# A two-block transformer on one core: the expert stage's banks, row fetches and weight pieces, and one more weight panel

## The chip, the cores and the metric

The kernel runs on one core of a Trainium2 chip. The metric is the device time of one execution in microseconds (us), lower is better; of several runs the median counts.

## The reference, cut to what matters

Two blocks work on 512 tokens of 1024 numbers, in float32. The first is attention of four kinds and a feed-forward layer. The second is a recurrent branch, a sparse attention branch, a cross attention and, last, a layer of 32 experts; then a final norm. The change touches the first product of the second block, `rmsnorm(h) @ w_in`, and the expert layer with all that follows:

```
p_grp, grp  = top_k(softmax(xt @ w_rg + b_rg), 1)          # one group of four
p_e, e_loc  = top_k(softmax(e_logits of that group), 2)    # two experts of its eight
gate        = p_grp * p_e / sum(p_e)
hid = silu(xb @ w_gate[e]) * (xb @ w_up[e])                # 1024 -> 512, xb: the rows routed to e
y[token] += (hid @ w_down[e]) * gate                       # 512 -> 1024
out = rmsnorm(h + y, norm_final)
```

Each of 512 tokens goes to two experts, so there are 1024 routed rows.

## The kernel before, in words

The code is one Python program that writes out every instruction. A scheduler orders the instructions of each engine when the kernel is built, by the program's order and by when its own model has an instruction's inputs and buffers ready; on the chip each engine then runs its own list in that order, and waits where an input is late. All weight loads are issued by SyncE (SP).

**Panels.** Outside the experts a float32 matrix product is made of three products of split numbers (`mm3`, lines 131 to 135). `panel` (line 106) loads 512 KB of weights in two pieces into `wraw` (three buffers in the pool `wp`, line 124), and splits each piece into a high part (ScalarE, line 125) and a low part (VectorE or GpSimd, line 128), which go to a tile `w`. The pool `wp` has three `w` tiles; another pool, `fw`, has two, which `panel` takes when `filling` is set; with `last=True` it takes the pool named in `self.wx`.

**The second block begins** in `rwkv_prep` (line 1218). `fm_halves` (line 158) makes four panels of `w2f`, and then multiplies them by the first 256 tokens, all four, and after that by the other 256. Each panel is 24 matmuls of 256 columns a half. The fourth panel's `w` tile is a `wp` tile that the first panel holds until its second half is done. Behind the four follow the panels of `mix(12)` and `mix(13)`.

**Router and slots.** `Router` finds each token's two experts block by block of 128 tokens: `R` (line 1858) is the token's place in its expert's list of up to 64, `A` and `Gt` are choice and gate. `full` counts experts that overflow, `gates` (line 1871) makes `Gt`. Then `Slots` (line 1937) is made: `ti` holds token numbers, gates and norm factors, in split parts. `gather(n)` for a pair of experts compares `R` with the place numbers (`OH`, line 1954, four VectorE operations), multiplies `OH` with `ti` (line 1959, four matmuls of 68 columns), turns the first column into a row number (lines 1961 to 1964; a place that is not taken becomes row 0), fetches 128 rows of 4 KB by an indirect DMA of GpSimd (line 1966), and copies gates and factors (lines 1970 to 1975). The first two pairs' rows are fetched before the experts begin, the others two pairs ahead.

**Experts.** `Experts.load` (line 1908) loads one of an expert's six pieces of 1 MB as two DMAs of 512 KB (line 1919). There are 192 such pieces and 16 tiles for them (`MW_AT`), of four pools; a tile is loaded again when its matmuls are done. `moe` (line 1990) goes over 16 pairs of experts. Two experts work side by side on TensorE: each takes 64 of the 128 columns of the array, so the matmuls of lines 2008 and 2024 come as 128x64, two at a time. For one pair: gate and up, 64 matmuls of 512 columns into the two banks `f` (line 2008); `silu_mul` (ScalarE line 1894, VectorE lines 1895 and 1896) makes `hid`; four transposes (line 2014, 128x128) and a copy make `hT`; the down product, 2 x 16 matmuls into `s` (line 2024), each half then scaled by the gate into `yhi` and `ylo` (lines 2027, 2028); eight transposes of the next pair's rows (line 1985). After every second pair the results are scattered to the tokens: eight sums of four matmuls 128x128 by 512 columns (line 1934), in the banks `pv`, `acc`, `s`, `s`, each added to `x` by VectorE (line 2045).

**Banks.** PSUM has eight banks: `f` two, `s` two, `tp` two, `pv` one, `acc` one.

**The end.** The last scatter is joined with the final norm (lines 2053 to 2075): two chains, each for two token blocks, of squares, a reciprocal root (`rsqrt`, line 192), products and stores.

Of the kernel before, what the change touches and what calls it, by code (L numbers as in the profile page):

```python
# [13 lines left out]
I32 = mybir.dt.int32  # L14
# [31 lines left out]
class Core:  # L46
# [1171 lines left out]
def rwkv_prep(K, pool, hhi, hlo, Mt, VA, eC, xg, kbd, red, bvd):  # L1218
# [6 lines left out]
    first = K.fm_halves([a["w2f"][4 + i] for i in range(4)], ("f", "f", "acc", "s"), hhi, hlo)  # L1225
# [673 lines left out]
class Experts:  # L1899
# [8 lines left out]
    def load(self):  # L1908
        e, w = self.order[self.n]
        at = MW_AT[self.n % len(MW_AT)]  # L1910
        self.n += 1
        if at == "wp":
            t = self.K.wp.tile([P, 2, 1024], F32R, name="w", bufs=W0).bitcast(F32)
        elif at == "mm":
            t = self.pools[at].tile([P, 2, 1024], F32R, name="mw", bufs=4).bitcast(F32)
        else:
            t = self.pools[at].tile([P, 2, 1024], F32, name="mw", bufs=MW_AT.count(at))
        for h in range(2):
            (self.K.nc.gpsimd if self.n in SWQ else self.K.nc.sync).dma_start(t[:, h], self.K.a["wexp"][e * 6 + w, :, h * 1024:(h + 1) * 1024])
        return [t[:, h, c * 512:c * 512 + 512] for h in range(2) for c in range(2)]  # L1920
# [16 lines left out]
class Slots:  # L1937


    def __init__(self, K, keep, xnd, Gt, R, r4, pool, mc):  # L1940
        self.K, self.xnd, self.R, self.pool, self.mc = K, xnd, R, pool, mc
        nc = K.nc
        self.ti = ti = keep.tile([P, 4, 68], F32R, name="ti")
        nc.vector.tensor_copy(ti[:, :, 0:2], mc["tok2"].rearrange("p (b c) -> p b c", b=4))
        K.split(ti[:, :, 2:34], ti[:, :, 34:66], Gt)
        K.split(ti[:, :, 66:67], ti[:, :, 67:68], r4[:, :, None])
        self.ready = [self.gather(0), self.gather(1)]

    def gather(self, n):
        K, nc, pool = self.K, self.K.nc, self.pool  # L1950
        e0 = 2 * n
        OH = pool.tile([P, 4, P], F32R, name="OH", bufs=2)
        for b in range(4):
            nc.vector.tensor_tensor(OH[:, b].rearrange("p (e s) -> p e s", e=2),
                                    self.mc["iota64"][:, None, :].to_broadcast([P, 2, 64]),
                                    self.R[:, b, e0:e0 + 2, None].to_broadcast([P, 2, 64]), op=OP.is_equal)
        pt = K.acc("tp")
        for b in range(4):
            nc.tensor.matmul(pt[:, :68], OH[:, b], self.ti[:, b], start=b == 0, stop=b == 3)
        tg = K.sm.tile([P, 4], F32, name="tg")  # L1960
        nc.vector.tensor_copy(tg[:, 0:1], pt[:, 0:1])

        row = K.sm.tile([P, 1], I32, name="row")
        nc.vector.tensor_scalar(row, pt[:, 0:1], -1.0, 0.0, op0=OP.add, op1=OP.max)
        xs = pool.tile([P, D], F32, name="xs", bufs=2)
        nc.gpsimd.indirect_dma_start(xs, None, self.xnd, bass.IndirectOffsetOnAxis(ap=row[:, 0:1], axis=0))  # L1966
        for s in range(2):
            hs = slice(64 * s, 64 * s + 64)
            e = e0 + s
            nc.vector.tensor_copy(tg[hs, 1:2], pt[hs, 2 + e:3 + e])  # L1970
            nc.vector.tensor_add(tg[hs, 1:2], tg[hs, 1:2], pt[hs, 34 + e:35 + e])
        nc.vector.tensor_copy(tg[:, 2:3], pt[:, 66:67])
        nc.vector.tensor_add(tg[:, 2:3], tg[:, 2:3], pt[:, 67:68])
# [16 lines left out]
def moe(K, x, slots, weights, pool, mc, out):  # L1990
# [3 lines left out]
    for q in range(8):  # L1994
        for pr in range(2):
# [5 lines left out]
            G, U = K.acc("f"), K.acc("f")  # L2001
# [57 lines left out]
    os_ = [K.acc(t) for t in ("pv", "acc", "f", "f")]  # L2059
# [4 lines left out]
    for p in range(2):  # L2064
        for b in (2 * p, 2 * p + 1):
            nc.scalar.activation(j[:, h1], os_[b], AF.Square, accum_out=ss[:, b, 1:2])
        s = ss[:, 2 * p:2 * p + 2]
        nc.vector.tensor_add(s[:, :, 0], s[:, :, 0], s[:, :, 1])
        r = K.rsqrt(s[:, :, 0], 1.0 / D, 1e-6, 2)
        for i, b in enumerate((2 * p, 2 * p + 1)):  # L2070
            rows = out[b * P:(b + 1) * P]
            nc.scalar.activation(x[:, b, h0], x[:, b, h0], AF.Copy, scale=r[:, i:i + 1])
            nc.sync.dma_start(rows[:, h0], x[:, b, h0])
            nc.vector.scalar_tensor_tensor(x[:, b, h1], os_[b], r[:, i:i + 1], g[:, h1], op0=OP.mult, op1=OP.mult)
            nc.sync.dma_start(rows[:, h1], x[:, b, h1])
# [64 lines left out]
def block2(K, h3, xd, out):  # L2140
# [140 lines left out]
    weights = Experts(K, {"keep": keep, "mm": mp})  # L2281

# [41 lines left out]
    K.ws.close()  # L2324
    upto, ni = router.full(keep)
    Gt = router.gates(keep)
# [3 lines left out]
    slots = Slots(K, keep, xnd, Gt, router.R, r4, K.pool(E, "slots"), mc)  # L2330
# [65 lines left out]
```

## Time and profile before

| what | us |
|---|---|
| median of 3 runs (range) | 2228.69 (2226.29 to 2232.9) |
| the profiled execution, its own time | 2238.75 |
| its span on the core | 2237.0 |
| TensorE busy in that span | 2086.9 (93%) |

The profile is of one execution. Times in it count from the start of its span; what lies around the span is 1.75 us. Engines: PE is TensorE's matmul, PEld its weight load, DVE VectorE, ACT ScalarE, POOL GpSimd, SP SyncE; a q behind the name is the engine's own queue. `L135` is a line of the kernel before. PEclk is TensorE's granted clock as a share of full speed.

### The profile page before, as it was taken

To read this page: it belongs to the slowest core of one execution; us is meant where nothing else is said; L and a number is where in the kernel's file an instruction comes from. 1 tells how busy PE (TensorE), PEld (TensorE's weight loads), DVE (VectorE), ACT (ScalarE), POOL (GpSimd) and SP (SyncE) were. 2 spreads that over 40 slices of the span, in tenths; PEclk is the share of its full clock that TensorE was granted. 3 is DMA by queue.
4 is the path that set the end of the run, shared out by engine and by line. 5 is a ranking of instruction groups with operands and counts; after the bars stand their busy time and mean duration, and the time that the engine had idled before them with its cause. 6 is when DMAs were issued, how large, how long until landed. Compare 5 with 4: busy or idle time off the path is not lost.

```text
span 2237.0 us, 28592 instructions
## 1 busy us (share of the span) xinstructions
PE 2086.9 (93%) x10252; PEld 1476.5 (66%) x10252; DVE 1074.4 (48%) x2554; ACT 712.5 (32%) x1507; POOL 485.6 (22%) x391
## 2 busy tenths in 40 slices
PE   7999899998999999979988999999997999999997
PEld 5777676686888888867777867777875433333332
DVE  5272226427764545475877656555445322222223
ACT  4253334433353434234532235543441110000102
POOL 2312331233133222233331121232131000000000
PEclk9899999999999999999998799999998999999999
DMA  5512332256242332133334342485257999999994
GB/s 174 162 47 67 94 97 73 67 173 230 73 138 96 98 99 95 58 112 107 101 116 108 105 162 91 156 260 167 94 187 264 403 416 413 413 415 414 413 415 182
DMA packets 203370, 411.39 MB, mean 184 GB/s; under 512 B 49192, under 2 KB 67752, under 8 KB 203096
## 3 DMA queue, kind: packets, MB, share of 16 engines
q1 hardware_dynamic: 200632, 400.08, 51.0%
q0 software_dynamic: 2592, 9.44, 1.1%
q8 instruction: 82, 1.34, 0.3%
q14 instruction: 64, 0.52, 0.1%
HBM read 371.46 MB, written 33.13 MB: 181 GB/s over the span
## 4 chain that ended last, share of the span: by engine, by line
PE 68%; DVE 12%; DMA 7%; issue 3%; ACT 3%; POOL 2%; SPq 0%; DVEq 0%; ACTq 0%; POOLq 0%
PE f L135 23%; PE f L2008 10%; PE s L2024 6%; PE acc L135 6%; PE s L135 6%; PE tp L135 2%; POOL w L128 2%; PE pv L269 1%; PE tp L261 1%; PE s L1934 1%; DMA wraw<-w2f 1%; PE pv L135 1%; ACT w L125 1%; DMA wraw<-wout 1%; PE pv L1934 1%
## 5 line engine op out<-in xcount | busy, mean ns | idle before, releaser
L128 POOL TENSOR_TENSOR w<-wraw,w 128x512 fp32r<-128x512 f32 x310 | 407.2, 1325 | 1074.1 <-ACT w L125 962.0
L125 ACT CAST w<-wraw 128x512 fp32r<-128x512 f32 (+1 forms) x446 | 261.6, 617 | 242.2 <-issue 51.7
L135 PE MATMUL f<-hhi,w 128*128 128x512 f32 (+1 forms) x832 | 281.0, 410 | 2.0 <-ACT w L125 0.7
L128 DVE TENSOR_TENSOR w<-wraw,w 128x512 fp32r<-128x512 f32 (+1 forms) x136 | 116.3, 856 | 189.6 <-ACT w L125 186.5
L2008 PE MATMUL f<-mw,xT 128*64 128x512 f32 x832 | 206.8, 594 | 0.0
L135 PE MATMUL f<-h2hi,w 128*128 128x512 f32 (+1 forms) x672 | 203.7, 384 | 0.3 <-POOL w L128 0.3
L135 PEld LDWEIGHTS f<-hhi,w 128*128 128x128 f32 x832 | 161.8, 200 | 35.1 <-issue 3.2
L135 PE MATMUL acc<-hhi,w 128*128 128x512 f32 (+1 forms) x512 | 169.3, 398 | 4.9 <-ACT w L125 1.9
L135 PE MATMUL f<-hlo,w 128*128 128x512 f32 (+1 forms) x416 | 170.0, 409 | 0.2 <-DVE hlo L187 0.2
L2008 PEld LDWEIGHTS f<-mw,xT 128*64 128x64 f32 x832 | 65.5, 137 | 124.6 <-issue 117.7
L135 PEld LDWEIGHTS f<-h2hi,w 128*128 128x128 f32 x672 | 125.2, 188 | 25.6 <-POOL w L128 0.5
L135 PE MATMUL f<-h2lo,w 128*128 128x512 f32 (+1 forms) x336 | 129.0, 384 | 0.0
L2024 PE MATMUL s<-mw,hT 128*64 128x512 f32 x416 | 121.8, 600 | 3.3 <-ACT hT L174 1.9
L135 PEld LDWEIGHTS acc<-hhi,w 128*128 128x128 f32 x512 | 96.3, 191 | 28.5 <-issue 4.3
L1966 POOL DMA_INDIRECT xs<-xnd,row x16 | 15.2, 953 | 423.3 <-DVE wraw L2000 171.0
L135 PE MATMUL acc<-hlo,w 128*128 128x512 f32 (+1 forms) x256 | 101.3, 396 | 0.0
L135 PEld LDWEIGHTS f<-hlo,w 128*128 128x128 f32 x416 | 83.1, 200 | 16.2 <-issue 1.4
L1895 DVE SCALAR_TENSOR_TENSOR hid<-hid,f 128x512 f32<-128x512 f32 x16 | 11.0, 688 | 160.3 <-ACT hid L1894 160.3
L1894 ACT ACTIVATE hid<-f,tg 128x512 f32<-128x512 f32 x16 | 11.0, 688 | 204.1 <-PE f L2008 204.1
L2024 PEld LDWEIGHTS s<-mw,hT 128*64 128x64 f32 x416 | 33.2, 136 | 59.6 <-issue 51.5
L135 PEld LDWEIGHTS f<-h2lo,w 128*128 128x128 f32 x336 | 63.1, 188 | 12.3
L2027 ACT ACTIVATE yhi<-s,tg 128x512 fp32r<-128x512 f32 x32 | 22.0, 688 | 150.8 <-PE s L2024 150.8
(743 smaller groups left out, 3991.4 us busy)
## 6 DMA issues: line engine op xcount, KB each, us to landing
mw<-wexp SPq DMA_DIRECT2D x310, 512.0 KB
w<-wexp SPq DMA_DIRECT2D x72, 512.0 KB
wraw<-wup SPq DMA_DIRECT2D x88, 256.0 KB
wraw<-w2f SPq DMA_DIRECT2D x76, 256.0 KB
wraw<-wgate SPq DMA_DIRECT2D x64, 256.0 KB
wraw<-wdown SPq DMA_DIRECT2D x44, 256.0 KB
wraw<-w1f SPq DMA_DIRECT2D x40, 256.0 KB
gated<-gt SPq DMA_DIRECT2D x28, 256.0 KB
```

Of the source, the lines that this page charges most:

```text
L125: nc.scalar.copy(hi[:, s], raw)
L128: eng.tensor_sub(lo[:, s], raw, hi[:, s].bitcast(F32))
L135: self.nc.tensor.matmul(out, l, r, start=start and i == 0, stop=stop and i == 2)
L261: nc.tensor.transpose(pt[:, off:off + P], Pt[s][i][:, j * P:(j + 1) * P], K.ident)
L269: one = lambda s: nc.tensor.matmul(o[64 * s:64 * s + 64, j * P:], v_of(j, s), ptS[s][:, at[j]:at[j] + n], start=start and j == 0, stop=sto ...
L1894: nc.scalar.activation(t, G, AF.Tanh, scale=half)
L1895: nc.vector.scalar_tensor_tensor(t, t, 1.0, G, op0=OP.add, op1=OP.mult)
L1934: K.nc.tensor.matmul(o, CT[:, b * P:(b + 1) * P], y[:, hs], start=start and i == 0, stop=i == len(items) - 1)
L1966: nc.gpsimd.indirect_dma_start(xs, None, self.xnd, bass.IndirectOffsetOnAxis(ap=row[:, 0:1], axis=0))
L2008: nc.tensor.matmul(o[64 * s:64 * s + 64], xT[:, kk, 64 * s:64 * s + 64], ws[s][k], start=kk == 0, stop=kk == 7)
L2024: nc.tensor.matmul(o[64 * s:64 * s + 64], hT[:, c, 64 * s:64 * s + 64], ws[s][c], start=c == 0, stop=c == 3)
L2027: nc.scalar.activation(yhi[:, hs], o, AF.Copy, scale=tg[:, 1:2])
```

## The change

- `fm_halves` takes `extra`: the last panel or panels take their `w` tile from `K.wx`, which is set to `fw` around the call in `rwkv_prep`. The four panels no longer share three tiles.
- `Experts.load` issues one DMA of 1 MB in place of two of 512 KB.
- `Slots` is made before the router, in the pool `keep`; two row tiles are cleared by GpSimd. `first` runs after the last token block's `R`: the row numbers and the fetches of the first two pairs are issued, and only then are the gates made. A gather becomes `rows` (four matmuls of 2 columns, row number, fetch) and `scales` (four matmuls of 66 columns, gates and factors). `full` moves behind `first`.
- A place that is not taken gets a row number past the last row, and the fetch is told to leave such rows out.
- Gate and up take `f`, `f` for the first pair of two and `pv`, `acc` for the second; the eight scatter sums take the two `s` banks alone.
- The final norm becomes one chain for all four token blocks, with half of the first halves' products on GpSimd.

```diff
-    def fm_halves(self, srcs, tags, xhi, xlo):
-
-        pans = [self.panel(src, 1024) for src in srcs]
+    def fm_halves(self, srcs, tags, xhi, xlo, extra=0):
+
+        pans = [self.panel(src, 1024, last=i >= len(srcs) - extra) for i, src in enumerate(srcs)]
...
-    first = K.fm_halves([a["w2f"][4 + i] for i in range(4)], ("f", "f", "acc", "s"), hhi, hlo)
+    K.wx = K.fw
+    first = K.fm_halves([a["w2f"][4 + i] for i in range(4)], ("f", "f", "acc", "s"), hhi, hlo, 1)
+    K.wx = None, 0
...
-        for h in range(2):
-            (self.K.nc.gpsimd if self.n in SWQ else self.K.nc.sync).dma_start(t[:, h], self.K.a["wexp"][e * 6 + w, :, h * 1024:(h + 1) * 1024])
+        (self.K.nc.gpsimd if self.n in SWQ else self.K.nc.sync).dma_start(t.rearrange("p h c -> p (h c)"), self.K.a["wexp"][e * 6 + w])
...
-    def __init__(self, K, keep, xnd, Gt, R, r4, pool, mc):
+    def __init__(self, K, keep, xnd, mc):
...
-        self.ti = ti = keep.tile([P, 4, 68], F32R, name="ti")
-        nc.vector.tensor_copy(ti[:, :, 0:2], mc["tok2"].rearrange("p (b c) -> p b c", b=4))
-        K.split(ti[:, :, 2:34], ti[:, :, 34:66], Gt)
-        K.split(ti[:, :, 66:67], ti[:, :, 67:68], r4[:, :, None])
-        self.ready = [self.gather(0), self.gather(1)]
+        self.tok = keep.tile([P, 4, 2], F32R, name="tok")
+        nc.vector.tensor_copy(self.tok, mc["tok2"].rearrange("p (b c) -> p b c", b=4))
+        self.ti = keep.tile([P, 4, 66], F32R, name="ti")
+
+        self.xs = [keep.tile([P, D], F32, name="xs", bufs=2) for _ in range(2)]
+        for t in self.xs:
+            nc.gpsimd.memset(t, 0.0)
+
+    def first(self, R, Gt, r4):
+
+        self.R = R
+        rows = [self.rows(n) for n in range(2)]
+        K, ti = self.K, self.ti
+        K.split(ti[:, :, 0:32], ti[:, :, 32:64], Gt())
+        K.split(ti[:, :, 64:65], ti[:, :, 65:66], r4[:, :, None])
+        self.ready = [self.scales(*r) for r in rows]
 
     def gather(self, n):
+        return self.scales(*self.rows(n))
+
+    def rows(self, n):
...
         for b in range(4):
-            nc.tensor.matmul(pt[:, :68], OH[:, b], self.ti[:, b], start=b == 0, stop=b == 3)
+            nc.tensor.matmul(pt[:, :2], OH[:, b], self.tok[:, b], start=b == 0, stop=b == 3)
         tg = K.sm.tile([P, 4], F32, name="tg")
+        none = K.sm.tile([P, 1], F32, name="none")
+        nc.vector.tensor_scalar(none, pt[:, 0:1], 0.5, 2.0 * T, op0=OP.is_lt, op1=OP.mult)
+        row = K.sm.tile([P, 1], I32, name="row")
+        nc.vector.scalar_tensor_tensor(row, pt[:, 0:1], -1.0, none, op0=OP.add, op1=OP.add)
         nc.vector.tensor_copy(tg[:, 0:1], pt[:, 0:1])
-
-        row = K.sm.tile([P, 1], I32, name="row")
-        nc.vector.tensor_scalar(row, pt[:, 0:1], -1.0, 0.0, op0=OP.add, op1=OP.max)
-        xs = pool.tile([P, D], F32, name="xs", bufs=2)
-        nc.gpsimd.indirect_dma_start(xs, None, self.xnd, bass.IndirectOffsetOnAxis(ap=row[:, 0:1], axis=0))
+        xs = self.xs[n] if n < 2 else pool.tile([P, D], F32, name="xs", bufs=2)
+        nc.gpsimd.indirect_dma_start(xs, None, self.xnd, bass.IndirectOffsetOnAxis(ap=row[:, 0:1], axis=0),
+                                     bounds_check=T - 1, oob_is_err=False)
+        return n, OH, tg, xs
+
+    def scales(self, n, OH, tg, xs):
...
+        for b in range(4):
+            nc.tensor.matmul(pt[:, :66], OH[:, b], self.ti[:, b], start=b == 0, stop=b == 3)
...
-            G, U = K.acc("f"), K.acc("f")
+            G, U = (K.acc(t) for t in (("f", "f"), ("pv", "acc"))[pr])
...
-                    o = K.acc(("pv", "acc", "s", "s")[b])
+                    o = K.acc("s")
...
-    os_ = [K.acc(t) for t in ("pv", "acc", "f", "f")]
+    os_ = [K.acc(t) for t in ("f", "f", "pv", "acc")]
...
+    for b in range(4):
+        nc.scalar.activation(j[:, h1], os_[b], AF.Square, accum_out=ss[:, b, 1:2])
+    nc.vector.tensor_add(ss[:, :, 0], ss[:, :, 0], ss[:, :, 1])
+    r = K.rsqrt(ss[:, :, 0], 1.0 / D, 1e-6, 4)
...
     K.ws.close()
+    g = []
+    slots.first(router.R, lambda: g.append(router.gates(keep)) or g[0], r4)
+    Gt = g[0]
     upto, ni = router.full(keep)
-    Gt = router.gates(keep)
...
-    slots = Slots(K, keep, xnd, Gt, router.R, r4, K.pool(E, "slots"), mc)
```

## Rows read from the trace of the kernel before

**Rows 1.** The page: its span, and TensorE's busy time, share and instructions.

```profile
span 2237.0 us, 28592 instructions
...
PE 2086.9 (93%) x10252; PEld 1476.5 (66%) x10252; DVE 1074.4 (48%) x2554; ACT 712.5 (32%) x1507; POOL 485.6 (22%) x391
```

**Rows 2.** Windows: length, busy PE, PEld, DVE, ACT, POOL, PEclk, DMA share, GB/s.

```profile
2160.00:2180.00 20.00, 18.44 (x86) 6.32 (x82) 2.82 (x4) 1.55 (x3) 0.00 (x0) 1.00 1.03 416
...
2200.00:2220.00 20.00, 18.37 (x72) 6.23 (x70) 4.66 (x7) 4.45 (x10) 1.78 (x2) 1.00 0.05 22
```

**Rows 3.** Waits of the expert stage: total us, times, longest us.

```profile
PEld f L2008 <- DMA mw<-wexp: 8.6, 28, 0.8
...
PE tp L2014 <- DVE hid L1896: 11.0, 13, 0.9
```

**Rows 4.** The chain, expert stage, first period: start us, us, what.

```profile
1727.61 15.47 PE f L2008 x64
...
1745.34 7.09 PE s L2024 x32
```

**Rows 5.** The timeline of TensorE where the second period begins.

```profile
1784.11 13.95 PE L2008 MATMUL f<-mw,xT 128*64 128x512 f32 x64
```

**Rows 6.** The chain, a later period, from its first matmuls to the next's.

```profile
2029.78 1.00 PE f L2008 x2
...
2033.31 13.89 PE f L2008 x62
...
2047.23 0.76 DVE hid L1896
...
2049.47 1.07 PE s L2024 x2
...
2051.16 3.58 PE s L2024 x14
2054.74 0.46 PE tp L1959 x3
...
2095.86 13.89 PE f L2008 x62
```

**Rows 7.** The chain, the end of the kernel.

```profile
2218.17 3.59 PE s L2024 x14
...
2231.64 0.66 DVEq L2392
```

**Rows 8.** The timeline of TensorE as the second block begins; in brackets: idle before.

```profile
999.32 0.39 PE L135 MATMUL s<-hhi,w 128*128 128x256 f32 x1 [4.27 <-ACT w L125]
...
1001.88 0.80 PE L135 MATMUL s<-hhi,w 128*128 128x256 f32 x2 [1.71 <-POOL w L128]
```

**Rows 9.** Windows over line 135's matmuls there: PE, PEld, PEclk, DMA share, GB/s.

```profile
1001.85:1006.90 5.05, 5.02 (x23) 5.02 (x24) 0.50 0.56 188
1006.90:1013.90 7.00, 7.00 (x60) 7.00 (x59) 1.00 0.42 131
```

**Rows 10.** The timelines of ScalarE, then SyncE's queue, at the same place.

```profile
998.65 1.13 ACT L125 CAST w<-wraw 128x512 fp32r<-128x512 f32 x2
...
994.76 28.86 SPq L124 DMA_DIRECT2D wraw<-w2f  x17
```

**Rows 11.** The chain between router and experts.

```profile
1714.30 0.19 DVE Rexp L1858
...
1716.64 1.05 PE tp L1959 x4
...
1718.22 7.31 DMA xs<-xnd,row
```

**Rows 12.** The timeline of GpSimd: a memset of 128x1024 elsewhere in the kernel.

```profile
988.23 0.96 POOL L1254 MEMSET BD<- 128x1024 f32 x1 [8.97 <-PE tp L234]
```

**Rows 13.** A window in which one load with rows of 8 KB a partition lands.

```profile
1300.20:1302.40 2.20, 2.20 (x11) 1.79 (x10) 0.00 (x0) 0.00 (x0) 0.00 (x0) 1.00 1.04 433
```

**Rows 14.** Groups by line over the expert stage: VectorE's additions of scatter sums.

```profile
L2045 DVE TENSOR_TENSOR x<-x,s 128x512 f32<-128x512 f32 x32 | 21.6, 680 | 3.1 <-PE s L1934 3.1
```

More of the change, by code (lines that the diff above doesn't have):

```diff
@@ L1937 @@
 class Slots:
-    def __init__(self, K, keep, xnd, Gt, R, r4, pool, mc):
-        self.K, self.xnd, self.R, self.pool, self.mc = K, xnd, R, pool, mc
+    def __init__(self, K, keep, xnd, mc):
+        self.K, self.xnd, self.pool, self.mc = K, xnd, keep, mc
         nc = K.nc
-        self.ti = ti = keep.tile([P, 4, 68], F32R, name="ti")
-        nc.vector.tensor_copy(ti[:, :, 0:2], mc["tok2"].rearrange("p (b c) -> p b c", b=4))
-        K.split(ti[:, :, 2:34], ti[:, :, 34:66], Gt)
-        K.split(ti[:, :, 66:67], ti[:, :, 67:68], r4[:, :, None])
-        self.ready = [self.gather(0), self.gather(1)]
+        self.tok = keep.tile([P, 4, 2], F32R, name="tok")
[11 more added lines that the diff above has]
+        self.ready = [self.scales(*r) for r in rows]
     def gather(self, n):
+        return self.scales(*self.rows(n))
+    def rows(self, n):
         K, nc, pool = self.K, self.K.nc, self.pool
@@ L1953, in gather @@
         for b in range(4):
-            nc.vector.tensor_tensor(OH[:, b].rearrange("p (e s) -> p e s", e=2),
-                                    self.mc["iota64"][:, None, :].to_broadcast([P, 2, 64]),
-                                    self.R[:, b, e0:e0 + 2, None].to_broadcast([P, 2, 64]), op=OP.is_equal)
+            nc.vector.tensor_tensor(
+                OH[:, b].rearrange("p (e s) -> p e s", e=2), self.mc["iota64"][:, None, :].to_broadcast([P, 2, 64]),
+                self.R[:, b, e0:e0 + 2, None].to_broadcast([P, 2, 64]), op=OP.is_equal)
         pt = K.acc("tp")
         for b in range(4):
-            nc.tensor.matmul(pt[:, :68], OH[:, b], self.ti[:, b], start=b == 0, stop=b == 3)
+            nc.tensor.matmul(pt[:, :2], OH[:, b], self.tok[:, b], start=b == 0, stop=b == 3)
         tg = K.sm.tile([P, 4], F32, name="tg")
+        none = K.sm.tile([P, 1], F32, name="none")
+        nc.vector.tensor_scalar(none, pt[:, 0:1], 0.5, 2.0 * T, op0=OP.is_lt, op1=OP.mult)
+        row = K.sm.tile([P, 1], I32, name="row")
+        nc.vector.scalar_tensor_tensor(row, pt[:, 0:1], -1.0, none, op0=OP.add, op1=OP.add)
         nc.vector.tensor_copy(tg[:, 0:1], pt[:, 0:1])
-        row = K.sm.tile([P, 1], I32, name="row")
-        nc.vector.tensor_scalar(row, pt[:, 0:1], -1.0, 0.0, op0=OP.add, op1=OP.max)
-        xs = pool.tile([P, D], F32, name="xs", bufs=2)
-        nc.gpsimd.indirect_dma_start(xs, None, self.xnd, bass.IndirectOffsetOnAxis(ap=row[:, 0:1], axis=0))
+        xs = self.xs[n] if n < 2 else pool.tile([P, D], F32, name="xs", bufs=2)
[3 more added lines that the diff above has]
+    def scales(self, n, OH, tg, xs):
+        K, nc = self.K, self.K.nc
+        e0 = 2 * n
+        pt = K.acc("tp")
+        for b in range(4):
+            nc.tensor.matmul(pt[:, :66], OH[:, b], self.ti[:, b], start=b == 0, stop=b == 3)
         for s in range(2):
@@ L1969, in gather @@
             e = e0 + s
[L1970 to L1973, printed above, removed]
+            nc.vector.tensor_copy(tg[hs, 1:2], pt[hs, e:1 + e])
+            nc.vector.tensor_add(tg[hs, 1:2], tg[hs, 1:2], pt[hs, 32 + e:33 + e])
+        nc.vector.tensor_copy(tg[:, 2:3], pt[:, 64:65])
+        nc.vector.tensor_add(tg[:, 2:3], tg[:, 2:3], pt[:, 65:66])
         nc.vector.scalar_tensor_tensor(tg[:, 3:4], tg[:, 2:3], 0.5, tg[:, 2:3], op0=OP.mult, op1=OP.mult)
@@ L2063, in moe @@
         scatter(K, os_[b], parts, b, h1, False)
[L2064 to L2075, printed above, removed]
+    for b in range(4):
+        nc.scalar.activation(j[:, h1], os_[b], AF.Square, accum_out=ss[:, b, 1:2])
+    nc.vector.tensor_add(ss[:, :, 0], ss[:, :, 0], ss[:, :, 1])
+    r = K.rsqrt(ss[:, :, 0], 1.0 / D, 1e-6, 4)
+    for b in range(4):
+        rows = out[b * P:(b + 1) * P]
+        nc.vector.scalar_tensor_tensor(x[:, b, h1], os_[b], r[:, b:b + 1], g[:, h1], op0=OP.mult, op1=OP.mult)
+        nc.sync.dma_start(rows[:, h1], x[:, b, h1])
+        if b % 2:
+            nc.gpsimd.tensor_scalar(x[:, b, h0], x[:, b, h0], r[:, b:b + 1], None, op0=OP.mult)
+        else:
+            nc.scalar.activation(x[:, b, h0], x[:, b, h0], AF.Copy, scale=r[:, b:b + 1])
+        nc.sync.dma_start(rows[:, h0], x[:, b, h0])
 def moe_rest(K, x, r4, gT, Gt, R, upto, ni, hnd):
@@ L2281, in block2 @@
     weights = Experts(K, {"keep": keep, "mm": mp})
+    slots = Slots(K, keep, xnd, mc)
     ss = rt.tile([P, 4, 2], F32, name="ssr")
```

## The prediction

> **What bounds the kernel now.** I read the page first. TensorE is busy 93% of a span of 2237.0 us [rows 1], and the chain that ended last runs mostly over it. So a part of the change pays where it fills a hole of TensorE, or shortens what it executes; a transfer that nothing waits for pays nothing. The change has two places: the start of the second block (about 950 to 1015 us) and the expert stage with its run-up (1640 us to the end).
>
> In the windows of the expert stage the 16 DMA engines look like the bound: their share is 1.03 at 416 GB/s, as it is from 1740 us on [rows 2]. The waits say otherwise. In the whole stage only TensorE's weight loads ever wait for an expert transfer, 28 times, 8.6 us in all and never over 0.8 us, and they run beside matmuls [rows 3]. In the chain the 62 or 64 gate and up matmuls of a pair take 15.5 us the first time and 13.9 us after that [rows 4 to 6], with no hole. Transfers have ended by about 2201 us (22 GB/s over the last window is 0.44 MB, one us of the rate before) [rows 2], and the last 14 expert matmuls begin at 2218.17 [rows 7]: the stream is 17 us ahead of its use. TensorE's own list is the bound, and the stream is just fast enough.
>
> What does that list lose? The first period of two pairs runs from 1727.61 to 1784.11, 56.5 us [rows 4, 5]; a later one from 2033.31 to 2095.86, 62.55 us, with the same work [rows 6]. In the first the 32 down matmuls of a pair are one run of 7.09 us [rows 4]. In the later one they are cut: two matmuls take 1.07 us, then 14 take 3.58 [rows 6], with transposes and scatter matmuls between. Two gate matmuls inside a run take 2 x 13.89/62 = 0.45 us; two of them alone, ahead of a scatter matmul, take 1.00 [rows 6]. So each time the half-width expert matmuls stop for full-width ones TensorE loses some 0.5 us, and something again on the way back. Between the first and last row of that group the chain makes this change ten times, in the first period four times: 6.05 us over 6 is about 1.0 us for a round trip.
>
> **The change part by part.**
>
> *Fourth panel.* TensorE stands still for 4.27 us before the first matmul of panel four and 1.71 us soon after [rows 8]; what follows runs at a granted clock of 0.50, the 1.2 GHz level, for 5.05 us, where 23 matmuls ran against 60 in the next 7.00 us at 1.00 [rows 9]: 2.3 of the 5.05 us are lost to the level that the engine fell to after the hole. Panel four's two casts start on ScalarE only at 998.65 [rows 10], since its tile came free only when the first panel was done, as the hole began at 999.32 - 4.27 = 995.05. With a tile of its own the hole goes: 4.27 + 1.71 + 2.3 = 8.3 us at most. Next late are the two pieces of `mix(12)`: SP issues loads one every 28.86/17 = 1.7 us from 994.76 [rows 10], with the order of ScalarE's casts behind them. I take 6 us, and keep 0 and 8.3 as ends.
>
> *First rows ahead of the gates.* After the last `R` at 1714.30 the old gather waits for the gates until 1716.64, multiplies for 1.05 us, and its rows land 7.31 us after 1718.22 [rows 11]. The new one needs only its last comparison; I take 1.4 us for that. With half its rows, and no later weights ahead of it, the fetch may be 1 to 2 us shorter: 3 us in all, ends 0 and 5. Behind it the gates come some 0.5 us later on VectorE, and with them the tiles of the pool `mw2`, which are needed a pair later. GpSimd gets two memsets of 0.96 us [rows 12] ahead of the output projection's splits: 0 to 1.9 us, I take 1.
>
> *Empty rows, 1 MB pieces.* 1024 of 2048 places are taken, so the 14 fetches inside the stage move 14 x 0.26 = 3.7 MB less, 8.9 us of the stream at 416 GB/s. For pieces with 8 KB rows the nearest row is a load that reached 433 GB/s at a share of 1.04 [rows 13] against 416 [rows 2]: 0 to 4% of about 460 us, 0 to 18 us. Nothing of it is on the path while TensorE's list holds it: I take 0. It is cover, and lets TensorE run ahead by 17 + 9 us or more before the stream binds. The Trainium skill would put more on this part: *DMA: Bandwidth & Descriptors*, section Bandwidth, says "Batch DMAs to ≥1 MiB for ≥75% of peak", and gives 2.0 us a DMA on top of its bytes. Worked out from that page, an estimate, 192 DMAs fewer would shorten the stream by up to 384 us if they came one after another; the trace does not agree, as pieces of 512 KB keep the engines at a share of 1.03.
>
> *Two pairs of banks.* Today the next pair's gate matmuls need the banks that `silu_mul` still reads. After the last gate matmul TensorE waits for VectorE's 0.76 us and the transposes [rows 6]; 13 such waits are 11.0 us [rows 3]. With other banks the next pair's matmuls can stand there, in the same half-width mode, at no change of width: 0.83 x 15 = 12.5 us. Against it, a gather has four more matmuls; three of the old ones took 0.46 us on the path [rows 6], so up to 0.6 us each time, and I take 0.37 x 14 = 5.2 us. Net 7.3 us. The ends are in the number of width changes, which the scheduler chooses anew: that is for the rivals.
>
> *Scatter banks, final norm.* Two `s` banks for eight sums: VectorE's addition frees a bank in 0.68 us [rows 14], while the other bank takes its four matmuls, so two banks just do; what it costs if not is rival B. The new end has the same operations in one chain, the last store's input being ready at about 2231.6 now [rows 7]: plus or minus 0.5 us, I take 0.
>
> *Sum.* -6 - 3 + 1 - 7.3 = -15.3 us; rounded, since the parts are no better, 16. The profiled execution took 2238.75 us with 1.75 us around its span, 10.06 us over the median of the runs (2226.29 to 2232.9). It would take 2222.7, and the median 2228.69 - 16 = 2212.7 us.
>
> **The rivals.**
>
> *A: the list loses its cuts.* With the next pair's half-width matmuls always ready, the scheduler has less reason to put full-width ones between. If the seven periods behind the first cost 56.5 us as the first did, 7 x 6.05 = 42 us go; the stream, 17 + 9 + 0 to 18 us to spare, then binds in between, so about 34 us here, in place of 7.3, with 8 us from the other parts: 2187 us. For it: the first period. Against: the cuts arose in a list with ready gate matmuls too.
>
> *B: slower, by scatter on two banks.* The eight sums now share `s`, `s` with the down product, whose last half holds a bank until ScalarE and VectorE have scaled it. Where a sum must wait, the scheduler has a filler at hand, half-width gate matmuls, and each insertion is a width change of 1.0 us. One for every two sums is 32 in all, 32 us, against 15 gained: +17, 2246 us. It decides from about 15 insertions on. For it: the 1.00 us row. Against: four banks today also have such gaps, with one or two insertions a period. The Trainium skill has the rule under this: *TensorEngine Tiling (Array Packing)*, Key Properties, "Mode switching requires drain". The trace agrees, with 1.00 us for two matmuls that take 0.45 in a run.
>
> *C: the list stays.* The holes are refilled with cut runs and the extra matmuls eat the rest; only parts of the first two items remain: 4 us, 2225 us, not to be told from no change. That empty rows are fetched after all, or that the 1 MB pieces are no faster, also lands here, as neither was counted.
>
> **How the numbers follow.** A change within 0.3%, 6.7 us, is about what a measurement of this kernel can't tell from none. Chances: forecast 0.46, A 0.23, C 0.18, B 0.13. The forecast's own range is 2202 to 2222, nearly all of it faster by over 6.7 us. Faster takes it and A, with a little of C: 0.71; same takes most of C: 0.16; slower takes B: 0.13. The range runs from A's 2187 to 2230, which leaves out about half of A's faster side and B.
>
> **What would show each step.** Right: no hole before panel four's first matmul and a granted clock of 1.00 there; the row fetch issued at least a us sooner after the last `R`; 13 waits on `hid` gone from TensorE; transfers that end earlier than 2201 us and further ahead of their use. A: four or five width changes a period, not ten. B: more than ten, scatter matmuls each followed by two gate matmuls. The forecast is wrong if expert matmuls wait for transfers, since then the stream binds, or if the later periods stay at 62 us.

## The result, and the profile after

| | us |
|---|---|
| after, median of 6 runs (range) | 2250.66 (2245.97 to 2263.13) |
| before, beside it, median of 6 runs (range) | 2228.24 (2226.29 to 2240.38) |
| ratio, 95% interval | 1.0088 (1.0062 to 1.0113) |
| profiled execution after, its span | 2247.0, 2245.2 |

The change makes the kernel slower by 0.9%, some 20 us. 2212.7 us was forecast, with a range up to 2230. In the page of after (busy us, share, count), TensorE is as busy as before [rows 1], in a longer span:

```profile
PE 2086.8 (93%) x10316; PEld 1476.6 (66%) x10316; DVE 1082.7 (48%) x2557; ACT 710.3 (32%) x1505; POOL 490.6 (22%) x394
```

The time was read stretch by stretch. In the table, **A** runs from the first matmul on `hhi` in `fm_halves` to the first `ztmp`, a tile of the recurrent branch; **B** from there to the last `Rexp`, the instruction that makes the last token block's `R`; **C** to the first gate matmul; **D** from there to the end of the last down matmul; **E** to the end of the span. B is the same code in all kernels but for six small matmuls of a gather, two memsets and when the first experts' weights are loaded. "Cuts" are the changes from half-width to full-width matmuls in D. Each row is one profiled execution, in us; the ratio comes from the timed runs. Differences in the text are taken before rounding.

| kernel | A | B | C | D | E | cuts | ratio to before |
|---|---|---|---|---|---|---|---|
| before | 162.1 | 580.2 | 13.3 | 494.1 | 15.2 | 72 | 1 |
| after | 157.8 | 581.5 | 14.9 | 508.7 | 17.4 | 70 | 1.0088 |
| e1 old banks | 158.3 | 585.9 | 15.0 | 494.5 | 17.4 | 70 | 1.0040 (1.0013 to 1.0067) |
| e2 one gather | 158.1 | 588.9 | 15.5 | 500.3 | 17.4 | 68 | 1.0064 (1.0038 to 1.0089) |
| e3 old end | 157.8 | 585.8 | 14.9 | 509.6 | 15.3 | 70 | 1.0075 (1.0047 to 1.0103) |
| e4 `extra` = 0 | 158.0 | 584.5 | 15.1 | 508.4 | 17.4 | 70 | 1.0105 (1.0064 to 1.0146) |
| e5 list written out | 157.8 | 588.9 | 15.0 | 470.7 | 15.2 | 34 | 0.9886 (0.9849 to 0.9922) |
| e6 without the losers | 160.4 | 585.7 | 14.9 | 487.2 | 15.3 | 67 | 0.9978 (0.9950 to 1.0006) |
| e7 before + panel | 157.7 | 577.5 | 12.6 | 494.6 | 15.2 | 72 | 1.0012 (0.9986 to 1.0037) |
| e8 before + 1 MB pieces | 162.1 | 585.5 | 14.0 | 494.9 | 15.1 | 73 | 1.0017 (0.9991 to 1.0043) |
| e9 e5, old transfers | 157.7 | 586.1 | 12.8 | 489.7 | 15.7 | 34 | 0.9982 (0.9963 to 1.0000) |
| e10 e5, branch, lora | 152.5 | 580.1 | 15.2 | 470.6 | 15.2 | 34 | 0.9878 (0.9846 to 0.9910) |
| e11 old sum banks | 162.8 | 586.2 | 14.8 | 497.9 | 17.4 | 68 | 1.0052 (1.0026 to 1.0077) |
| e12 old gate banks | 163.2 | 592.2 | 15.7 | 509.3 | 17.4 | 70 | 1.0112 (1.0078 to 1.0146) |
| e13 e5, old pieces | 158.0 | 584.1 | 11.7 | 481.8 | 15.8 | 34 | 0.9948 (0.9923 to 0.9974) |
| e14 e5, all rows | 162.9 | 584.7 | 14.2 | 478.9 | 15.2 | 34 | 0.9960 (0.9935 to 0.9985) |

After against before: -4.3 in A, +1.3 in B, +1.5 in C, +14.5 in D, +2.2 in E, together +15.2 us. What lies ahead of A took 965.0 us after and 972.0 before, and 956.5 to 973.7 in all kernels; so the two profiled spans are only 8.2 us apart. B shows how far one execution can be trusted over a long stretch: nearly the same code took 577.5 to 592.2 us at a mean granted clock of 0.93 to 0.95. D repeats better: where the stage is the same code it took 494.1 and 494.6 (before, e7), 508.4 to 509.6 (after, e3, e4), 470.7 and 470.6 (e5, e10). So small parts are judged in their own stretch, and totals by ratios.

**The stage (D).** The waits of after (us in total, times, longest) answer to [rows 3]:

```profile
PEld s L1935 <- DVE x L2072: 21.0, 40, 1.5
PE tp L2041 <- DVE hid L1898: 13.7, 16, 0.9
```

PEld is TensorE's weight load. Over the same whole stage of before, which is longer than the window of [rows 3], the wait on `hid` was this:

```profile
PE tp L2014 <- DVE hid L1896: 12.7, 15, 0.9
```

So the waits on `hid` have not gone, and the scatter's weight loads wait 40 times for VectorE's additions. SP's queue in the same stage of after:

```profile
SPq L1920 <- PE s L2051: 158.0, 43, 6.8
SPq L1920 <- DMA mw<-wexp: 2.9, 3, 2.1
```

Loads wait for TensorE to free tiles, hardly for transfers, and the stream ends earlier than in [rows 2] (window, PE, PEld, DVE, ACT, POOL busy, clock, DMA share, GB/s):

```profile
2180.00:2200.00 20.00, 17.33 (x66) 5.83 (x63) 7.06 (x11) 1.37 (x2) 0.00 (x0) 1.00 0.37 153
2200.00:2220.00 20.00, 17.66 (x74) 5.67 (x73) 1.44 (x2) 1.27 (x2) 0.00 (x0) 1.00 0.00 1
```

TensorE's list is still the bound, and it has become longer. Of the 14.5 us, 6.0 lie in the last period of two pairs (73.1 us for 67.1) and 3.6 in the second; the later ones between took 63.5 us each, for 62.6. By the time from each matmul to the next, the gathers take 14.8 us for 8.8, the scatter 75.1 for 67.8. The timeline shows why the scatter does, here at one of its blocks:

```profile
1892.70 1.07 PE L2051 MATMUL s<-mw,hT 128*64 128x512 f32 x2
1893.09 0.74 DVE L2055 SCALAR_TENSOR_TENSOR ylo<-s,tg,yhi 128x512 fp32r<-128x512 f32 x1
1893.97 0.47 PE L1935 MATMUL s<-yhi,wraw 128*128 128x512 f32 x1 [0.19 <-DVE ylo L2055]
...
1895.03 0.28 DVE L1970 TENSOR_TENSOR OH<-mciota,Rexp 128x128 fp32r<-128x128 f32 x1
...
1895.49 0.68 DVE L2072 TENSOR_TENSOR x<-x,s 128x512 f32<-128x512 f32 x1
1896.22 0.50 PE L1935 MATMUL s<-yhi,wraw 128*128 128x512 f32 x1 [1.09 <-DVE x L2072]
1896.65 3.65 PE L2051 MATMUL s<-mw,hT 128*64 128x512 f32 x14
```

One `s` bank is taken by the second half of the down product, begun at 1892.70. The first sum has the other. Its last matmul starts at 1894.74, but VectorE has the next gather's comparisons and copies ahead of the addition, which starts at 1895.49, and the second sum waits 1.09 us. Five periods show this hole at the same place.

The wait on `hid` stays for a reason that the next lines show (the list of one pair, from its `hid` to the next pair's gate matmuls):

```profile
1796.07 0.66 PE L2041 MATMUL tp<-ident,hid 128*128 128x128 f32 x4 [0.84 <-DVE hid L1898]
1796.56 0.60 PE L2012 MATMUL tp<-ident,xs 128*128 128x128 f32 x4
...
1804.53 0.66 PE L2012 MATMUL tp<-ident,xs 128*128 128x128 f32 x4
1804.94 0.58 PE L1975 MATMUL tp<-tok,OH 128*128 128x2 f32 x4
1805.45 1.07 PE L2035 MATMUL pv<-mw,xT 128*64 128x512 f32 x2
```

The next pair's gate matmuls have a free bank, but not their input: `xT` is complete only after the eighth row transpose, at 1804.53, behind `hid` and the down product.

**The other stretches.** The hole before panel four [rows 8] is gone, and another stands before `mix(12)`. In C, the row transposes wait twice, 4.46 and 3.54 us; before, they waited once, for the rows [rows 11]. In E, the joined chain ends for all four blocks at 2235.4, and the first store is issued at 2237.21, 9.5 us after the last down matmul's end (2227.76); before it was 7.1 us (2221.75 to 2228.81). Three pieces of the timeline of after:

```profile
1005.46 0.80 PE L135 MATMUL acc<-hhi,w 128*128 128x512 f32 x1 [7.21 <-DVE ks L1233]
```

```profile
1713.42 1.72 PE L2012 MATMUL tp<-ident,xs 128*128 128x128 f32 x7 [4.46 <-PEq L2115]
1718.68 0.48 PE L2012 MATMUL tp<-ident,xs 128*128 128x128 f32 x1 [3.54 <-issue]
1719.09 2.83 PE L2035 MATMUL f<-w,xT 128*64 128x512 f32 x6
```

```profile
2235.61 3.11 POOL L2100 TENSOR_SCALAR x<-x,ny 128x512 f32<-128x512 f32 x2 [6.42 <-DVE ny L209]
...
2237.21 0.34 SPq L2103 DMA_DIRECT2D out<-x  x1
...
2241.08 0.60 SPq L2103 DMA_DIRECT2D out<-x  x1
```

### The profile page after: what moved, and what is told of

Its sections match the earlier page's. It is cut to its first block, busy times and chain, and to the rows that moved or that the text cites. A ratio compares the mean times of both kernels' runs of the same rounds, so it can differ in the third digit from the quotient of the medians.

```text
span 2245.2 us, 28556 instructions
## 1 busy us (share of the span) xinstructions
PE 2086.8 (93%) x10316; PEld 1476.6 (66%) x10316; DVE 1082.7 (48%) x2557; ACT 710.3 (32%) x1505; POOL 490.6 (22%) x394
## 5 line engine op out<-in xcount | busy, mean ns | idle before, releaser
L2035 PE MATMUL f<-mw,xT 128*64 128x512 f32 x416 | 101.9, 594 | 0.0
L2035 PEld LDWEIGHTS f<-mw,xT 128*64 128x64 f32 x416 | 32.3, 137 | 62.4 <-issue 62.4
L996 DVE SCALAR_TENSOR_TENSOR cv<-f,cw,cv 128x511 f32<-128x511 f32 x41 | 30.7, 750 | 67.3 <-ACT cv L995 67.3
L2035 PE MATMUL acc<-mw,xT 128*64 128x512 f32 x224 | 62.3, 593 | 0.0
```

The costliest lines, as they stand in the source:

```text
L996: nc.vector.scalar_tensor_tensor(t[:, 1:], u[:, :T - 1], c[:, 1:2], t[:, 1:], op0=OP.mult, op1=OP.add)
L2035: nc.tensor.matmul(o[64 * s:64 * s + 64], xT[:, kk, 64 * s:64 * s + 64], ws[s][k], start=kk == 0, stop=kk == 7)
```

## The experiments

All timed against before; their rows stand in the table above.

### Banks: e1, e11, e12

e12 is the kernel after with the first of these edits, e11 with the second, e1 with both.

```diff
-            G, U = (K.acc(t) for t in (("f", "f"), ("pv", "acc"))[pr])
+            G, U = K.acc("f"), K.acc("f")
```

```diff
-                    o = K.acc("s")
+                    o = K.acc(("pv", "acc", "s", "s")[b])
```

> The kernel after with the old banks alone: gate and up in the two f banks for every pair, the eight sums in pv, acc, s, s. My theory: two banks for the sums make TensorE wait for VectorE's addition (9 holes of 7.6 us between scatter matmuls, none before), and the second pair of gate banks fills nothing, since the wait on hid is 16 x, 13.7 us, against 15 x, 12.7 us. So this is 7 us below the kernel after, about 2243 to 2244; the holes inside the scatter are gone; the wait on hid stays at 12 to 14 us. Rival, the price lies in the order of the list, not in banks: the number of changes from half-width to full-width matmuls falls only by one, so the time stays within 2 us of the kernel after. Rival, the gate banks do work: the wait on hid grows, and the gain is below 4 us.

> The kernel after with the sums in pv, acc, s, s again, gate and up still in two pairs of banks. My theory: all of what the banks cost lies in the two s banks, so this has most of the gain of the old banks (stage 493.9 us against 508.1): a stage of 490 to 497 us, no holes between scatter matmuls, and the wait on hid still there, 12 us or more, as the next pair's gate matmuls have no xT. Rival: pv and acc, now shared by gates and sums, collide, and the stage stays above 500 us. Rival: the wait on hid is filled, and the stage falls below 487 us.

> The kernel after with gate and up in the two f banks again, the sums still in the two s banks. My theory: the second pair of gate banks does nothing, so the time is that of the kernel after within 2 us, stage 508 us, wait on hid 13 to 14 us. Rival: the second pair of banks was worth its forecast, and the stage grows by 5 us or more.

The four kernels give D for each pairing:

| D, us | gates in `f` | gates in two pairs |
|---|---|---|
| sums in four banks | 494.5 (e1) | 497.9 (e11) |
| sums in `s` alone | 509.3 (e12) | 508.7 (after) |

The two `s` banks cost 10.7 to 14.8 us, more than the 7.6 us of holes behind VectorE's additions that the expectation counted: besides them, the list around them changes (gate and up matmuls take 248.6 us in e1, 251.0 in after). The second pair of gate banks gives nothing in either row, and where sums use `pv` and `acc` too it costs 3.4 us. TensorE's waits in e1, and then in e11:

```profile
PE tp L2041 <- DVE hid L1898: 12.9, 15, 0.9
```

```profile
PE tp L2041 <- DVE hid L1898: 13.1, 16, 0.9
PE pv L1935 <- DVE hid L1897: 4.9, 6, 1.5
```

The wait on `hid` is nearly the same with either choice, and in e11 sums wait for the gates' bank. No run has both the second pair of gate banks and an `xT` made early, so what the banks would be worth then is open.

### Gather, end, panel: e2, e3, e4, e7

e2, e3 and e4 are the kernel after with one of these edits each:

```diff
-            nc.tensor.matmul(pt[:, :2], OH[:, b], self.tok[:, b], start=b == 0, stop=b == 3)
+            nc.tensor.matmul(pt[:, :2 if n < 2 else 68], OH[:, b], (self.tok if n < 2 else self.ti)[:, b], start=b == 0, stop=b == 3)
```

```diff
-    r = K.rsqrt(ss[:, :, 0], 1.0 / D, 1e-6, 4)
+    for p in range(2):
...
+        r = K.rsqrt(s[:, :, 0], 1.0 / D, 1e-6, 2)
```

```diff
-    first = K.fm_halves([a["w2f"][4 + i] for i in range(4)], ("f", "f", "acc", "s"), hhi, hlo, 1)
+    first = K.fm_halves([a["w2f"][4 + i] for i in range(4)], ("f", "f", "acc", "s"), hhi, hlo, 0)
```

e7 is the kernel before with the change's edits to `fm_halves` and its call alone.

> The kernel after with one product of 68 columns for each gather inside the stage, as before; the first two pairs keep the split form. My theory: the split costs 14 groups of four matmuls more, 14.8 us in all against 8.8 us, so this is 6 us below the kernel after, about 2244 to 2245. Rival, the extra matmuls stand in holes that would be there anyway: no change (within 2 us), and the wait that they filled appears in their place (before the down product, on the copy of hid).

> The kernel after with the old end: two chains, each for two token blocks, and no product on GpSimd. My theory: the joined chain holds all stores until the fourth block's squares are summed, 17.4 us from the last down matmul to the end against 15.2 us, so this is 2.2 us below the kernel after, and the stores begin 2 us or more earlier. Rival, the end is set by the last store's own latency: within 0.5 us of the kernel after in the stretch from the last down matmul to the end.

> The kernel after with the first product of the second block as before: the fourth panel waits for a tile that the first one holds. My theory: the fourth panel is worth the 4.3 us by which the first ztmp stands nearer to the first matmul on hhi (157.8 against 162.1 us), not the 6 us forecast, since the hole moved to mix(12) (7.2 us, waiting for a bank that ScalarE's mix frees late). So this is 4 us above the kernel after, about 2255. Rival, the stage is held by what comes behind it: within 1.5 us. Rival, the whole 8.3 us of holes and low clock were won: 8 us above.

> The kernel before with the fourth panel alone (the wider rotation of tiles, which K.wx sets for all panels of that stretch, and the extra panel). Setting only the count of extra panels back changed nothing in the run before, since the rotation gives the fourth panel a tile of the other pool all the same. My theory: 4 us below before, with 158 us from the first matmul on hhi to the first ztmp against 162, and a hole of 7 us before mix(12). Rival: 8 us below, the whole of the holes and of the low clock; or nothing.

e2: D falls by 8.3 us, 6.0 of it in the gathers. e3: E falls by 2.1 us, as expected; it takes back the joined chain and GpSimd's products together. e4, expected 4 us slower, undid nothing: `K.wx` also widens the rotation of tiles (line 118), so that the fourth panel gets another pool's tile with `extra` at 0 too. e7 is the test: A falls by 4.4 us. The gain isn't safe: of 13 kernels that have the panel with the old lora order, nine show 157.7 to 158.3, but e11, e12 and e14 are back at 162.8 to 163.2, and e6 is between.

The gain is not that of a filled hole either: the holes were 4.27 and 1.71 us [rows 8], and the new one is 7.21. From 45 us behind A's start on, the windows (length, busy times, clock, DMA share, GB/s) of before, after, e6 and e11 are these:

```profile
1017.03:1134.13 117.10, 109.58 (x561) 87.00 (x560) 75.45 (x119) 52.24 (x93) 35.01 (x33) 0.96 0.37 106
1009.96:1122.74 112.78, 105.73 (x564) 83.88 (x563) 74.59 (x118) 51.52 (x92) 34.94 (x32) 1.00 0.37 107
1006.45:1121.82 115.37, 108.61 (x565) 86.19 (x564) 74.80 (x118) 52.09 (x93) 35.21 (x33) 0.97 0.37 106
1004.59:1122.37 117.78, 111.02 (x564) 88.01 (x563) 74.82 (x118) 51.61 (x93) 34.97 (x32) 0.95 0.36 103
```

All four have 561 to 565 matmuls of A left there. They differ in the granted clock, 1.00 in the nine kernels, 0.97 in e6, 0.95 in e11, e12 and e14 and 0.96 before, and the time follows it. Why the clock differs among kernels with the same panel stays open. The ratio of e7 can't tell 4 us from none.

### The list written out: e5, e6

```diff
-            slots.ready.pop(0)
-            nxt = slots.ready[0][0], slots.turned(slots.ready[0][1], pool)
...
+            with K.tc.issue_after(last.ins):
+                nxt = slots.ready[0][0], slots.turned(slots.ready[0][1], pool, (0,))
...
+            with K.tc.issue_after(last.ins):
+                slots.turned(slots.ready[0][1], pool, (1,), nxt[1])
```

Both have e1's, e2's and e3's edits. e5 also names, for gates, gather and scatter, the TensorE instruction that each stands behind; `(0,)` and `(1,)` are the halves of the row transposes, ahead of and behind those of `hid`.

> The kernel after with the old banks, one product of 68 columns a gather inside the stage, the old end, and TensorE's list in the expert stage written out: for each pair 64 gate and up matmuls, four transposes of the next pair's rows, the four of hid, four more of rows, 32 down matmuls, the gather, and behind every second pair all scatter matmuls at once. 33 changes from half to full width in place of 72, and a filler for the wait on hid. My theory (TensorE's list bounds the stage, each such change costs 0.52 us by the time to the next matmul, and the wait on hid of 0.83 us can be filled only by work whose input is there): 39 x 0.52 = 20 us and 15 x 0.67 = 10 us below the 493.6 us of before, so a stage of about 463 us and a time of about 2228 - 30 - 4 (panel) = 2195 us; fewer if the way back costs too, down to a stage of 445 us. Rival, the stream binds: 176 MB behind the first 16 pieces at 433 GB/s are 426 us, and rows 10 us, so that a stage under 445 us is out of reach and gate matmuls wait for transfers; if pieces come as they did before (420 GB/s and gaps), the stage stays above 480 us. Rival, cuts cost nothing: 2215 us or more.

> The kernel after with the old banks, one product of 68 columns a gather inside the stage, and the old end: what is left of the change is the fourth panel, the first rows ahead of the gates, the empty rows and the pieces of 1 MB. The order is the scheduler's own (65 changes of width against 71). My theory: what is left gains 4 us by the panel, nothing by rows and pieces, about 0 by the first rows (2.2 us sooner fetched, 1.6 us later used), and up to 3 us by six changes of width: 2221 to 2226 us. Rival, pieces or skipped rows cost or gain something in the stage: outside of 2215 to 2230 us.

e6 is not told from before by its ratio. Its D is 6.9 us shorter than before's. Five cuts fewer are some 2.5 us of that by the price below; what makes the rest is open, since no run has the left-out rows alone with the scheduler's list. e5 is 1.1% faster than before, beyond both kernels, though its stage is 8 us longer than expected. Its list at one pair, and at a later one:

```profile
1757.90 0.66 PE L2016 MATMUL tp<-ident,xs 128*128 128x128 f32 x4
1758.84 0.66 PE L2053 MATMUL tp<-ident,hid 128*128 128x128 f32 x4 [0.29 <-DVE hid L1898]
1759.34 0.60 PE L2016 MATMUL tp<-ident,xs 128*128 128x128 f32 x4
1760.28 7.09 PE L2066 MATMUL s<-mw,hT 128*64 128x512 f32 x32 [0.34 <-DVE hT L178]
```

```profile
2034.47 4.10 PE L2042 MATMUL f<-mw,xT 128*64 128x512 f32 x16 [0.54 <-DMA mw<-wexp]
2040.11 3.65 PE L2042 MATMUL f<-mw,xT 128*64 128x512 f32 x16 [1.54 <-DMA mw<-wexp]
2045.10 3.65 PE L2042 MATMUL f<-mw,xT 128*64 128x512 f32 x14 [1.34 <-DMA mw<-wexp]
```

The hole of 0.84 us has become 0.29 (15 of them 4.2 us), and the down matmuls are one run again. From 1920 us on gate matmuls wait for transfers, 10 times, 12.3 us: now the stream binds. Against e6 the list itself, without these waits, is 16.5 + 12.3 = 28.8 us shorter. Other holes, most of them at `hid` (12.9 us in e6, 5.1 here), make 11 us of it. If the remaining 18 us are all put down to the 33 cuts fewer, a cut costs about 0.5 us, an estimate. The Trainium skill's "Mode switching requires drain" (*TensorEngine Tiling (Array Packing)*, Key Properties) agrees in kind.

### The transfers: e8, e9, e13, e14

e8 is the kernel before with the change's edit to `load` alone. e13 is e5 with the first of these edits, e14 with the second, e9 with both.

```diff
-        (self.K.nc.gpsimd if self.n in SWQ else self.K.nc.sync).dma_start(t.rearrange("p h c -> p (h c)"), self.K.a["wexp"][e * 6 + w])
+        for h in range(2):
+            (self.K.nc.gpsimd if self.n in SWQ else self.K.nc.sync).dma_start(t[:, h], self.K.a["wexp"][e * 6 + w, :, h * 1024:(h + 1) * 1024])
```

```diff
-        nc.vector.scalar_tensor_tensor(row, pt[:, 0:1], -1.0, none, op0=OP.add, op1=OP.add)
+        nc.vector.tensor_scalar(row, pt[:, 0:1], -1.0, 0.0, op0=OP.add, op1=OP.max)
...
-                                     bounds_check=T - 1, oob_is_err=False)
```

> The kernel before with pieces of 1 MB alone. My theory: TensorE's list bounds the stage, so the time is that of before within 3 us, with transfers that run further ahead (SP waiting for TensorE to free tiles, and not for transfers). Rival, the stream bounds the stage: up to 4% of 460 us, 5 to 18 us faster. Rival, larger pieces come late where a tile is waited for: slower by 3 us or more, with more waits of weight loads on transfers than 28.

> The kernel with the written-out list, but with the transfers of the kernel before: pieces of 512 KB, and row 0 fetched for places that are not taken. With the written-out list gate matmuls waited 10 times, 12.3 us, for transfers, so the stream binds there. My theory: empty rows and pieces were cover, worth nothing while TensorE's list bound the stage (8 pieces alone: 1.0017), and are worth what they save once it does not: 14 x 0.26 MB at 420 GB/s are 8.9 us, the pieces 0 to 10 us more. So 9 to 15 us above the written-out list, with holes before gate matmuls of 20 us or more. Rival: the waits come from the order of loads, not from the rate, and the time is within 3 us of the written-out list.

> The written-out list with pieces of 512 KB, empty rows still left out. Both old transfers together made the stage 18.9 us longer (489.65 against 470.71 us). My theory: the empty rows are 14 x 0.26 MB, 8.9 us at 420 GB/s, and the pieces the other 10 us, so the stage is 479 to 482 us here. Rival: the pieces are all of it, 488 us or more; or nothing, 472 us or less. For the hole of 3.5 us ahead of the eighth row transpose (0.74 us with both old transfers): if it comes with the 1 MB pieces, which the 16 KB packet of the instruction queue would stand behind, it is 1 us or less here and the way from the last Rexp to the first gate matmul is 13 us; if it comes with the left-out rows, it stays at 3.5 us, and the way at 15 us.

> The written-out list with pieces of 1 MB, and row 0 fetched for places that are not taken. My theory: the stage is 8.9 us longer than with the rows left out, 478 to 481 us. Rival: rows cost nothing, since they lie in gaps of the stream, 472 us or less. For the hole ahead of the eighth row transpose: the other way about, 3.5 us here if it comes with the pieces, 1 us or less if it comes with the left-out rows.

With the scheduler's list, pieces of 1 MB are worth nothing (e8, D +0.8 us). With the written-out list, old pieces cost 11.1 us of D (e13), rows that nobody needs 8.2 (e14), both together 18.9 (e9): they add up. Rows that are left out are not moved: the queue of GpSimd's fetches (packets, MB, share) before, and then after:

```profile
q0 software_dynamic: 2592, 9.44, 1.1%
q0 software_dynamic: 2448, 5.25, 0.6%
```

The windows of e5 and then of e13 show the rate of the stream:

```profile
1900.00:2100.00 200.00, 187.19 (x849) 79.17 (x846) 57.78 (x170) 19.59 (x30) 7.56 (x7) 1.00 1.01 420
```

```profile
1900.00:2100.00 200.00, 184.03 (x816) 76.00 (x814) 56.28 (x168) 19.03 (x29) 7.56 (x7) 1.00 1.03 408
```

420 against 408 GB/s, 2.9%, with the DMA share above 1.0 in both. The Trainium skill (*DMA: Bandwidth & Descriptors*, Bandwidth) points the right way with its batches of 1 MiB, but the size by the trace is 3% here.

C answers the second question of the last two expectations, what the hole ahead of the eighth row transpose comes with. With 512 KB C is 11.7 and 12.8 us (e13, e9), with 1 MB 15.0 and 14.2 (e5, e14). The timeline of e13:

```profile
1712.75 1.73 PE L2017 MATMUL tp<-ident,xs 128*128 128x128 f32 x7 [4.24 <-DVE OH L1973]
1715.06 0.47 PE L2017 MATMUL tp<-ident,xs 128*128 128x128 f32 x1 [0.59 <-issue]
```

The hole before the eighth transpose is 0.59 us here, 0.74 in e9, 1.13 in e14 (where the rows themselves land later) and 3.47 in e5: it takes both changes together. Counted from the start of the last `Rexp`, a packet of 16 KB of the instruction queue starts after 8.8, 10.2, 11.1 and 12.3 us in the same order, and the eighth transpose starts 1.3 to 1.5 us after that packet's end in each. That TensorE waits there for code, which both changes together delay, fits these profiles; it was argued, not tried by itself.

### Branch and lora: e10

```diff
+    upto, ni = router.full(keep)
     g = []
...
-    upto, ni = router.full(keep)
```

To e5 this adds the edit shown, and the loop that makes `lora` and `lolo` is moved from ahead of `mix(12)` to behind the `ks` loop.

> The kernel with the written-out list and two things more, each read at its own place. First, the count of full experts stands ahead of the first rows again, so that the branch that reads it can come early. My theory: TensorE's first row transposes wait for that branch (4.5 us and then 3.5 us in the kernel after), so the way from the last Rexp to the first gate matmul falls from 15.05 us to 11 to 13 us. Rival: the wait is code or rows arriving, and the way stays at 15 us, or gets longer since the row numbers come after the count. Second, the loads and casts of the low-rank weights stand behind the ks loop. My theory: the hole of 7.2 us before mix(12) is ScalarE's queue, in which the mixes of the first panels stand behind a cast that waits for its load, so the hole falls to 3 us or less and the way from the first matmul on hhi to the first ztmp from 157.8 to 153 to 155 us. Rival: the hole is the panel of mix(12) itself, and stays.

C stays at 15.2 us: the branch was not the cause. A falls to 152.5 us, and of the hole before `mix(12)` this is left:

```profile
991.02 0.50 PE L135 MATMUL acc<-hhi,w 128*128 128x512 f32 x1 [0.44 <-DVE ks L1233]
```

So the hole of 7.2 us was ScalarE's queue, in which `mix` stood behind a cast of `lora` whose load was late. ScalarE's rows of after:

```profile
990.67 0.62 ACT L1243 CAST lora<-g 128x512 fp32r<-128x512 f32 x1 [5.29 <-DMA g<-rw_w2a]
996.45 0.62 ACT L1243 CAST lora<-g 128x512 fp32r<-128x512 f32 x1 [5.16 <-DMA g<-rw_w2a]
...
998.52 0.68 ACT L1232 ACTIVATE ks<-f,ppd 128x512 f32<-128x512 f32 x1
```

Before, the same cast stood ahead of panel four's two casts, which began at 998.65 [rows 10]:

```profile
998.13 0.62 ACT L1241 CAST lora<-g 128x512 fp32r<-128x512 f32 x1 [9.00 <-DMA g<-rw_w2a]
```

By the semaphores that panel four's cast waits for, its loads had landed at 992.0 and its tile was free by 994.0, a us before the hole began; from then on it stood behind `lora` alone. With a tile of its own its casts went ahead of `lora`, and `mix` stood behind in their place. The edit of e10 was not tried on the kernel before. A falls by less than the hole did, as another one opens in e10 behind `mix(12)`, for which the trace names no releaser:

```profile
1018.68 0.77 PE L1276 MATMUL tp<-wa,lora 128*128 128x512 f32 x1 [5.22 <-issue]
```

With 2202.25 us e10 is the fastest kernel, though not told from e5 by ratio.

## Why the prediction was wrong

The side was wrong. Step by step:

- **What bounds the kernel**: right. TensorE's list binds before and after (e8: no gain from larger pieces). The price of a cut, 1.0 us, was about twice too high: some 0.5 by e5 against e6.
- **Two pairs of banks, -12.5 us**: the step that failed first. "With other banks the next pair's matmuls can stand there" looked at the bank alone. Their other input, `xT`, was not made yet. The holes ahead of the transposes of `hid` went from 15 of 12.7 us to 16 of 13.7; they shrank only when work with its inputs ready was put there (e5).
- **Scatter banks, 0**: the step that cost most, 10.7 to 14.8 us (e11, e1). "The other bank takes its four matmuls, so two banks just do" counted two free banks and an idle VectorE. The down product held one, and VectorE had the gather's operations ahead of the addition. Rival B named this place, but as inserted gate matmuls; cuts fell from 72 to 70, and TensorE waited instead. That its 2246 us lie near the measured time is luck.
- **Split gather, +5.2**: near in size, 6.0 us by the gathers, 8.3 us of D in e2.
- **Fourth panel, -6**: -4.3 in A, the size near, the reason not. The tile was not what held panel four: it was free by 994.0, and ScalarE's cast of `lora` stood ahead of the panel's casts until 998.65. What is late next was named (`mix(12)`, ScalarE's casts), but its hole of 7.2 us, longer than the two that went, was not priced. What was won came later in A, at a clock of 1.00 in place of 0.96, and three kernels with the same panel did not have it.
- **First rows, -3, memsets, +1**: the fetch is issued 2.2 us sooner, yet C is 1.5 us longer in after. With old pieces it is 1.6 us shorter than before (e13). The loss comes with the 1 MB pieces, most of it only where rows are left out too, and I had no term for it here. The memsets take 1.85 us of GpSimd at 1636 us, in B, which can't show a microsecond.
- **Empty rows and pieces, 0**: right for the pieces with this list (e8); for the rows with this list no run shows it by itself. As terms of a stream that binds, rows 8.9 us (measured 8.2) and pieces 0 to 18 (11.1) were right too.
- **Final norm, 0**: +2.2 us. One chain holds every store until the last block's squares are in. "The same operations in one chain" looked at the last store's input, and not at the first store.
- **Rival A**: the cuts didn't vanish by themselves. When most of them were removed by hand, the stream bound the stage as A had it, at 470.7 us rather than 460.

## What to carry to other kernels

A free buffer fills a hole only if all other inputs of the work meant for it are ready at that place in the list: look up the producer of each. Count free banks where they are used, with who holds them there and what stands ahead of the releasing operation on its engine. When a buffer looks like the reason for a hole, read the queue of the engine that fills it as well: here a cast that waited for its load stood in front. A saving on transfers such as the larger pieces is cover as long as the compute list binds, and pays once that list is shortened; so shorten the list first, by naming the order where a scheduler cuts runs.

## What was not expected of the hardware

One DMA of 1 MB in place of two of 512 KB raised a stream that already kept the DMA share above 1.0 from 408 to 420 GB/s. The same pieces came with 1.3 to 3.4 us more between router and experts (C: e14 against e9, e5 against e13), where a hole ends 1.3 to 1.5 us behind an instruction packet. And the end of A, with the same matmuls, took 5 us more at a granted clock of 0.95 (e11) than at 1.00 (after), though the two kernels differ only in code that runs far behind it.
